# Third buffer of split weights, shared solve tiles, merge evictions after the weights, solved blocks copied on VectorE

## The chip, the cores and the metric

The kernel runs on one core of a Trainium2 chip. The metric is the device time of one execution in microseconds (us); three runs of the kernel before took 4509.4 to 4517.8 us, median 4514.72. Engines: PE is TensorE (PEld its weight loads), DVE VectorE, ACT ScalarE, POOL GpSimd, SP SyncE, which here issues most transfers.

## The reference, cut to what matters

Two layers over 256 context and 512 latent tokens of width 1024. Each layer has a mixer (one projection into three branches, a merge of the branches, an output projection) and an MLP. In the last layer only the latent tokens come out.

```
z = modulate(x) @ w_in                      # 10112 columns
A: r,k,v,decay,a = ...shifted, LoRA...      # RWKV-7, two directions, 16 heads of 64
   S = S*w_t - (S kk_t)(kk_t a_t)^T + v_t k_t^T;  y_t = S r_t
B: silu(layer_norm(depthwise_conv31(a * sigmoid(b))))
C: GQA, 8 query and 2 key heads of 128, softmax over context and latent keys
out = sum(sigmoid(z_gate) * (branch @ w_branch)) @ w_out
x = x + gate * rms_norm(out);  x = x + gate * rms_norm(relu(h @ w1)**2 @ w2)
```

## The kernel before

All matrices are float32. A product with a weight is made as three products of rounded parts. `weight_half` (L369) loads 512 rows by 128 columns of a weight into `raw`, ACT rounds it into a high part `wh` (L328), and the rest `raw - wh` becomes `wl`, on DVE (L332) or, in most of the mixer, on POOL (L330). Then `hh*wh + hl*wh + hh*wl` is summed in PSUM (`mm`). `raw` has two buffers (`nraw`), `wh` and `wl` have `nw` buffers.

In the mixer such products are jobs of eight steps in a queue; `fill` (L396, L412) takes out the next steps. The RWKV branch is written as generators, one yield per step, which `weave` runs in turn, letting `fill` put job steps between. Job steps thus fill PE while the branch waits for other engines. When `fill` starts a new half of a weight, it first issues halves until `ready` holds two. The tile framework then reorders the instructions of each engine, by their dependencies and the order in which they were issued; each engine runs its list in order.

The branch handles heads in pairs, eight per layer. For one pair: `rw_keys` writes the keys `BK`; `rw_front` the decayed `KR` and the Gram blocks `GL`, `GB`; `rw_rest` the solve's right hand sides `KM`; `rw_solve` (L855 to L864) inverts the triangular 32 x 32 blocks of all chunks on DVE and writes them to `Z` with two transposes (L863, L864). `rw_merge` joins blocks of 32 to blocks of 64, for each direction: PE multiplies (L892), ACT evicts with a minus sign (L896), ACT copies the solved blocks masked into `TT`, a view of `GL` (L900), PE multiplies again (L904), ACT evicts into `TT` (L906). `rw_batch` applies `TT` (L920, L931), `rw_chain` runs over the twelve chunks, `rw_readout` writes the output. The next pair's preparation, `prep`, runs beside it; `rw_bonus` has a key product (L877), whose operand DVE makes (L871).

`stage` (`f0`, one buffer) holds a finished job's copy: for the token shift (L654, L658) or on its way to DRAM (L1073 to L1076). `att_stats` loads ten stored tiles into `BK`, `KM` and `GL` in the layer's last pair and squares them (L544).

Of the kernel before, what the change touches and what calls it, by code (L numbers as in the profile page):

```python
# [8 lines left out]
F32 = mybir.dt.float32  # L9
# [3 lines left out]
AF = mybir.ActivationFunctionType  # L13
ALU = mybir.AluOpType
# [4 lines left out]
D = 1024  # L19
KT = 8  # L20
SEQ = 512
CTX = 256
TOK = CTX + SEQ
# [13 lines left out]
ROWS = (slice(0, 64), slice(64, 128))  # L37
# [39 lines left out]
class Kern:  # L77
# [247 lines left out]

    def split(s, hi, lo, src, pool=False):
        nc = s.nc
        nc.scalar.activation(out=hi, in_=src, func=AF.Copy)  # L328
        if pool:
            nc.gpsimd.tensor_tensor(out=lo, in0=src, in1=hi.bitcast(F32), op=ALU.subtract)  # L330
        else:
            nc.vector.tensor_tensor(out=lo, in0=src, in1=hi.bitcast(F32), op=ALU.subtract)  # L332
# [64 lines left out]
    def fill(s, n=1):  # L397
        nc = s.nc
        for _ in range(min(n, len(s.jobs))):
            k, mh, ml, T, done, pre = s.jobs.pop(0)  # L400
            if k % 4 == 0:
                while s.halves and len(s.ready) < 2:
                    s.ready.append(s.weight_half(*s.halves.pop(0)))
                s.cur = s.ready.pop(0)
            if k == 0:
                s.jps = s.mm()
                s.jctx = (pre(),) if pre else ()
            wh, wl = s.cur
            for w, m, f in ((wh, mh, 0), (wh, ml, 1), (wl, mh, 2)):
                a = m(k)  # L410
                for b, t0, t1 in s.pieces(T):
                    ins = nc.tensor.matmul(s.jps[:, b, :t1 - t0], lhsT=w[:, k % 4, :], rhs=a[:, t0:t1], start=k == 0 and f == 0, stop=k == KT - 1 and f == 2)  # L412
                    if s.pin and f == 0 and b == 0:
                        s.tc.keep_in_program_order(ins)
            if k == KT - 1:
                done(s.jps, *s.jctx)
# [112 lines left out]
    def att_stats(s, T, hold):  # L529

        nc = s.nc
        rs = s.ars = s.cp.tile([128, 2, 10, 6], F32, tag="ars", name="ars", bufs=1)
        slots = []
        for n in (('BK', 0), ('BK', 1), ('KM', 0), ('KM', 1), ('GL', 0)):
            t = s.big[n]
            t = t.rearrange({3: "p a b -> p (a b)", 4: "p a b c -> p (a b c)", 5: "p a b c d -> p (a b c d)"}[len(t.shape)])
            slots += [t[:, c:c + TOK] for c in range(0, t.shape[1], TOK)]
        heads = [8, 9] + list(range(8))
        for j, z in zip(heads, slots):
            s.zload(z, j, TOK if j > 7 else T)  # L540
        yield from hold
        for j, z in zip(heads, slots):
            o = 0 if j > 7 else TOK - T
            nc.scalar.activation(out=z[:, o:], in_=z[:, o:], func=AF.Square)  # L544
            cps = s.g([128, 6])
            for t in range(o // 128, 6):
                nc.tensor.matmul(cps[:, t:t + 1], lhsT=z[:, t * 128:t * 128 + 128], rhs=s.ones, start=True, stop=True)
            nc.vector.tensor_copy(rs[:, 0, j, o // 128:], cps[:, o // 128:])
            yield 1.4
        n0 = (TOK - T) // 128  # L550
        for h, t0 in ((slice(0, 8), n0), (slice(8, 10), 0)):
            nc.vector.tensor_scalar(out=rs[:, 0, h, t0:], in0=rs[:, 0, h, t0:], scalar1=1.0 / 128, scalar2=EPS, op0=ALU.mult, op1=ALU.add)
            u = slots[0][:, 0:60].rearrange("p (a b) -> p a b", b=6)
            s.rsqrt(rs[:, 0, h, t0:], rs[:, 1, h, t0:], u[:, h, t0:])
        q0, q1 = rs[:, 0, 0:8, n0:], rs[:, 1, 0:8, n0:]
        nc.vector.tensor_scalar(out=q0, in0=q0, scalar1=ATT_SCALE, scalar2=None, op0=ALU.mult)
        nc.vector.tensor_scalar(out=q1, in0=q0, scalar1=-1.0, scalar2=None, op0=ALU.mult)
# [87 lines left out]
        s.in_job(l, c0, T, lambda ps: s.shift_done(P, c0, T, dst(), ps))  # L645

    def stage(s):
        return s.wp.tile([128, TOK], F32, tag="f0", name="f0", bufs=1)

    def shift_done(s, P, c0, T, dst, ps):  # L650
        nc = s.nc
# [230 lines left out]

    def rw_merge(s, Q, d):

        nc = s.nc
        GL = s.big['GL', d]
        Dn, Dt = (s.Z[:, i:i + 384].rearrange("p (u t) -> p u t", t=32) for i in (1152 * d, 768 - 384 * d))
        one, two, c = (HI, LO, 0) if d else (LO, HI, 32)
        xp = s.g([128, 12, 32])
        for q in range(12):  # L890
            for h in range(2):
                nc.tensor.matmul(xp[two[h], q, :], lhsT=GL[one[h], h, q, c:c + 32], rhs=Dn[one[h], q, :], start=True, stop=True)  # L892
        TT = Q['TT', d] = GL.rearrange("p h c t -> p (h c t)")[:, 0:768].rearrange("p (c t) -> p c t", t=64)
        Xn = Dn
        for h in range(2):
            nc.scalar.activation(out=Xn[two[h]], in_=xp[two[h]], func=AF.Copy, scale=-1.0)  # L896
        yield 1.1 + s.sched['merge']
        for h in range(2):
            for o, m in ((0, s.tlo), (32, s.thi)):
                nc.scalar.activation(out=TT[ROWS[h], :, o:o + 32], in_=Dt[ROWS[h]], func=AF.Copy, scale=m[ROWS[h]])  # L900
        tr = s.g([128, 12, 32])
        for q in range(12):
            for h in range(2):
                nc.tensor.matmul(tr[one[h], q, :], lhsT=Xn[two[h], q, :], rhs=Dt[two[h], q, :], start=True, stop=True)  # L904
        for h in range(2):
            nc.scalar.activation(out=TT[one[h], :, c:c + 32], in_=tr[one[h]], func=AF.Copy, scale=-0.5)  # L906
        yield 1.1 + s.sched['merge']
# [170 lines left out]

    def run(s):
        nc, tc, i = s.nc, s.tc, s.i  # L1080
        s.nraw, s.nw, s.lo_pool, s.turn = 2, 2, False, 0
        s.halves, s.ready, s.jobs = [], [], []
        s.cops, s.pin = [], False
        s.psum('gen')
# [12 lines left out]
        with ExitStack() as xc:  # L1097
            X = xc.enter_context(tc.tile_pool(name="x0", bufs=1)).tile([128, KT, TOK], F32, name="X")
            sp = xc.enter_context(tc.tile_pool(name="n0", bufs=1))
            s.load_x(sp, X)  # L1100
            ss = s.ps2()
# [8 lines left out]
        for l in range(DEPTH):  # L1110
            T = TOK if l < DEPTH - 1 else SEQ
# [15 lines left out]
    def rwkv_phase(s, l, P, T):  # L1127
        nc, tc = s.nc, s.tc
        s.psum('rw')
        s.lo_pool = False  # L1130
        with ExitStack() as rc:
# [7 lines left out]
            for a, b in lay[3]:  # L1139
# [4 lines left out]
            s.X = s.A[:, 0:1024].rearrange("p (a b) -> p a b", b=32)  # L1144
            s.big = {(n, d): s.rp.tile(sh, F32, name=f"{n}{d}") for d in range(2) for n, sh in (
                ('BK', [128, 12, 2, 64]), ('KR', [128, 2, 12, 64]), ('GL', [128, 2, 12, 64]),
                ('GB', [128, 2, 12, 2, 64]), ('UV', [128, 24, 64]), ('KM', [128, 12, 2, 64]))}
            lat = T != TOK
            F = s.sched = SCHED[l]
            s.tdebt, s.tratio = 0.0, F['tap0']  # L1150
# [7 lines left out]
            def chain(*gs):  # L1158
                for g in gs:
                    yield from g  # L1160
            def prep(p, I, Q, *held):

                return chain(s.after(I, 'k', 0, s.rw_kk(P, p, I)), *held, s.rw_decay(P, p, Q), s.rw_keys(P, p, I, Q, 0), s.rw_keys(P, p, I, Q, 1),
                             s.after(I, 'r', 0, s.rw_bonus(P, p, I, Q, T)))

            def grams(I, Q, part):

                a, b = ((0, 0), (1, 2), (2, 1))[part]
                c = [slice(0, 8), slice(8, 12)] if part == 1 else [slice(0, 4), slice(8, 12)]
                gs = [s.rw_front(I, Q, 0, a, lat), s.rw_front(I, Q, 1, b, lat)]  # L1170
                if part == 1:
                    gs.append(s.rw_seed(0, slice(0, 8)))
                if part == 2:
                    gs += [s.rw_seed(1, slice(0, 12)), s.rw_seed(0, slice(8, 12))]
                return chain(*gs)
# [3 lines left out]
            I, In = {}, {}  # L1179
            s.rw_inputs(l, P, 0, T, I, 'krv')  # L1180
            s.fill(24)
            Q = s.rw_open(l, 0)
            s.pin = False
            spills(F['early'])
            s.weave(F['open'], prep(0, I, Q))
            s.conv_jobs(l, P, 0, T, s.ocv)
            s.weave(F['end'], chain(*(grams(I, Q, k) for k in range(3))))
            Qn = s.rw_open(l, 1)
# [6 lines left out]
            for p in range(8):  # L1195
                ev = set()

                def wait(*ns):
                    while not ev.issuperset(ns):
                        yield 0.0  # L1200
# [13 lines left out]
                held = [s.rw_readout(l, P, p - 1, old, T, s.orw), note('ro')] if old else [note('ro')]  # L1214
                gs = [chain(s.rw_merge(Q, 0), s.rw_batch(Q, 0, lat), note('b0'), wait('b1'), s.rw_chain(Q, lat, ev.add, wait('ro'))),
                      chain(s.rw_merge(Q, 1), s.rw_batch(Q, 1, lat), note('b1'))]
                if more:
                    gs.append(chain(prep(p + 1, In, Qn, *held), wait('s3'), grams(In, Qn, 0), wait('s7'), grams(In, Qn, 1), wait('s11'), grams(In, Qn, 2)))
                else:
                    gs.append(chain(*held, wait('s11'), s.rw_readout(l, P, p, Q, T, s.orw)))  # L1220
                    gs.append(chain(wait('b0', 'b1'), s.att_stats(T, wait())))
                s.weave(F['first'] if more else F['last'], *gs)
                s.taps(len(s.cops))
                if more:
                    s.conv_jobs(l, P, p + 1, T, s.ocv)
                    I, old, Q, In = In, Q, Qn, {}
                    if p < 6:
                        Qn = s.rw_open(l, p + 2)
# [106 lines left out]
    def mlp_phase(s, l, PP, T, acc, actx):  # L1335

        nc, tc, i, P = s.nc, s.tc, s.i, PP[l]
        o = TOK - T
# [12 lines left out]
        with tc.tile_pool(name="mlp", bufs=1) as sp:  # L1351
# [26 lines left out]
            if not last:  # L1378
                s.mod_pre(PP[l + 1])
                s.mod_post(PP[l + 1])  # L1380
            s.R = s.rstd(sp, ss, T, 1.0 / D, 0, CTX)
        with tc.tile_pool(name="n2", bufs=1) as sp:
            if last:
                s.post_norm(sp, acc, X, s.R, T, P['gm'][1], lambda k: None)
# [62 lines left out]
```

## Time and profile before

| | |
|---|---|
| profiled execution | 4503.07 us, span 4501.3 us |
| three runs | 4509.4, 4514.72, 4517.8 us |
| busy share of the span | PE 93%, PEld 76%, DVE 59%, ACT 42%, POOL 18% |
| granted PE clock, mean | 0.956 |
| mixer of layer 0, of layer 1 | about 130 to 1390 us, 2530 to 3710 us |

A row of waits says which engine sat idle before which line, and whose work ended the wait. In rows in order of time, the bracket is the idle time of the engine just before and who ended it. [...]

### The profile page before, as it was taken

The page shows a single profiled execution, that of the slowest core. Times are in us where ns is not written, and L with a number is a line of the kernel's source. Part 1 is how long each engine was busy: PE and PEld are TensorE (multiplying, and loading weights), DVE is VectorE, ACT ScalarE, POOL GpSimd, SP SyncE. Part 2 cuts the span into 40 slices and gives each one's busy share as a digit, 9 for nine tenths or more (in the row PEclk, how much of TensorE's full clock was granted, in tenths as well). Part 3 has the DMA queues.
Part 4 walks back from the last instruction along what each step waited for, and adds up shares of the span by engine and source line. Part 5 has one row for each costly group of instructions (what it writes and reads, how often), then busy time and mean ns, then how long its engine had stood idle before and what let it go on. Part 6 is the DMA issues. An engine that isn't in the chain of part 4 may idle for free. (4 is left out here: it accounts for less than half of the span.)

```text
span 4501.3 us, 76922 instructions
## 1 busy us (share of the span) xinstructions
PE 4197.0 (93%) x31232; PEld 3411.4 (76%) x31232; DVE 2642.9 (59%) x4762; ACT 1889.5 (42%) x3690; POOL 831.3 (18%) x737
## 2 busy tenths in 40 slices
PE   6999999999998989899999899999999988898998
PEld 4888888888786668689999667877777775475886
DVE  3788788887855443132233568778787845443344
ACT  3455445444534442232223354555555534434333
POOL 0011221212112144300000102122122212262001
PEclk8999999999999999999999889999999979998998
DMA  4211111111224234343322221111111223142332
GB/s 161 62 47 53 57 58 57 51 52 58 73 84 157 71 110 142 126 141 117 107 87 63 69 61 52 50 60 47 56 54 57 75 71 121 57 133 64 96 96 82
DMA packets 438346, 364.05 MB, mean 81 GB/s; under 512 B 19022, under 2 KB 386792, under 8 KB 431848
## 3 DMA queue, kind: packets, MB, share of 16 engines
q1 hardware_dynamic: 417256, 279.43, 20.5%
q10 hardware_dynamic: 20736, 79.70, 4.9%
q8 instruction: 247, 4.05, 0.4%
q14 instruction: 107, 0.88, 0.1%
HBM read 299.29 MB, written 53.48 MB: 78 GB/s over the span
## 5 line engine op out<-in xcount | busy, mean ns | idle before, releaser
L328 ACT ACTIVATE wh<-raw 128x512 fp32r<-128x512 f32 x700 | 441.4, 631 | 1261.5 <-PE mm L389 558.3
L330 POOL TENSOR_TENSOR wl<-raw,wh 128x512 fp32r<-128x512 f32 x388 | 535.5, 1381 | 2062.3 <-ACT wh L328 1699.1
L412 PE MATMUL mm<-hh,wh 128*128 128x384 f32 (+1 forms) x2072 | 668.6, 381 | 49.4 <-ACT wh L328 40.7
L412 PE MATMUL mm<-hl,wh 128*128 128x384 f32 (+1 forms) x2072 | 644.5, 370 | 7.0 <-POOL hl L330 7.0
L412 PE MATMUL mm<-hh,wl 128*128 128x384 f32 (+1 forms) x2072 | 641.4, 369 | 4.9 <-POOL wl L330 4.6
L332 DVE TENSOR_TENSOR wl<-raw,wh 128x512 fp32r<-128x512 f32 x312 | 215.5, 691 | 589.7 <-ACT wh L328 586.4
L412 PEld LDWEIGHTS mm<-hh,wh 128*128 128x128 f32 x2072 | 379.2, 195 | 112.7 <-ACT wh L328 45.6
L473 DVE SCALAR_TENSOR_TENSOR cv<-u,dw,cv 128x783 f32<-128x783 f32 (+1 forms) x480 | 458.3, 955 | 3.1
L412 PEld LDWEIGHTS mm<-hl,wh 128*128 128x128 f32 x2072 | 389.6, 195 | 47.7 <-issue 12.1
L412 PEld LDWEIGHTS mm<-hh,wl 128*128 128x128 f32 x2072 | 388.0, 194 | 47.1 <-POOL wl L330 10.8
L412 PE MATMUL mm<-oh,wh 128*128 128x384 f32 (+1 forms) x768 | 256.7, 389 | 12.1 <-DVE acc L1273 4.1
L412 PE MATMUL mm<-oh,wl 128*128 128x384 f32 (+1 forms) x768 | 245.9, 374 | 22.0 <-POOL wl L330 22.0
L412 PE MATMUL mm<-ol,wh 128*128 128x384 f32 (+1 forms) x768 | 243.5, 370 | 6.6 <-POOL ol L330 5.6
L389 PE MATMUL mm<-hh,wh 128*128 128x384 f32 (+1 forms) x768 | 239.3, 367 | 6.3 <-ACT hh L347 3.6
L389 PE MATMUL mm<-hl,wh 128*128 128x384 f32 (+1 forms) x768 | 238.3, 365 | 5.5 <-POOL hl L330 5.0
L389 PE MATMUL mm<-hh,wl 128*128 128x384 f32 (+1 forms) x768 | 236.0, 362 | 0.0
L389 PE MATMUL mm<-fh,wh 128*128 128x384 f32 (+1 forms) x768 | 230.2, 353 | 0.0
L389 PE MATMUL mm<-fh,wl 128*128 128x384 f32 (+1 forms) x768 | 230.0, 353 | 0.0
L389 PE MATMUL mm<-fl,wh 128*128 128x384 f32 (+1 forms) x768 | 229.8, 353 | 0.0
L862 DVE TENSOR_TENSOR A<-A,Z 128x30 f32<-128x30 f32 (+14 forms) x480 | 198.2, 413 | 15.8
L861 DVE TENSOR_TENSOR Z<-A 128x30 f32<-128x30 f32 (+14 forms) x480 | 190.7, 397 | 16.5
L412 PEld LDWEIGHTS mm<-oh,wh 128*128 128x128 f32 x768 | 143.9, 195 | 55.2 <-ACT wh L328 15.8
(294 smaller groups left out, 7425.6 us busy)
## 6 DMA issues: line engine op xcount, KB each, us to landing
raw<-in_w_in_dram SPq DMA_DIRECT2D x316, 256.0 KB
raw<-in_w_ff_dram SPq DMA_DIRECT2D x256, 256.0 KB
wmod<-in_w_mod_dram ACTq DMA_DIRECT2D x48, 1024.0 KB
raw<-in_w_branch_dram SPq DMA_DIRECT2D x96, 256.0 KB
z<-f ACTq DMA_DIRECT2D x40, 384.0 KB
gt<-z SPq DMA_DIRECT2D x24, 384.0 KB
raw<-in_w_out_dram SPq DMA_DIRECT2D x32, 256.0 KB
z<-f ACTq DMA_DIRECT2D x32, 256.0 KB
```

What stands on the lines that cost most here:

```text
L328: nc.scalar.activation(out=hi, in_=src, func=AF.Copy)
L330: nc.gpsimd.tensor_tensor(out=lo, in0=src, in1=hi.bitcast(F32), op=ALU.subtract)
L332: nc.vector.tensor_tensor(out=lo, in0=src, in1=hi.bitcast(F32), op=ALU.subtract)
L389: nc.tensor.matmul(ps[:, b, :t1 - t0], lhsT=w[:, k % 4, :], rhs=a[:, t0:t1], start=k == 0 and f == 0, stop=k == KT - 1 and f == 2)
L412: ins = nc.tensor.matmul(s.jps[:, b, :t1 - t0], lhsT=w[:, k % 4, :], rhs=a[:, t0:t1], start=k == 0 and f == 0, stop=k == KT - 1 and f == 2)
L473: s.tap_pin(nc.vector.scalar_tensor_tensor(out=hold['c'], in0=u[:, k:k + L], scalar=w(k), in1=hold['c'], op0=ALU.mult, op1=ALU.add))
L861: nc.vector.tensor_tensor(out=tm, in0=X[:, k + 1:, k:k + 1].to_broadcast([128, n, k]), in1=X[:, k:k + 1, 0:k].to_broadcast([128, n, k]), o ...
L862: nc.vector.tensor_tensor(out=X[:, k + 1:, 0:k], in0=X[:, k + 1:, 0:k], in1=tm, op=ALU.add)
```

## The change

`nw` is 3, and `fill` issues halves until `ready` holds `nw`. `split` keeps its last ACT instruction in `last_hi`; the evictions of a merge (now L895) get a dependency on it, which puts them behind it in ACT's order, without a semaphore. The masked copies into `TT` go from eight instructions of 64 partitions on ACT per pair to four of 128 partitions on DVE (L900 still). `KM` becomes the same tile as `BK`, and `prep` waits for each direction's batch (`b0`, `b1`) before it writes its keys; in a layer's first preparation that wait is empty. `stage` has two buffers. `att_stats` uses `BK`, `GL` and `A`. At the MLP's end the row of the norm uses the tag `sq`. Between `att_stats` and these copies, lines stand one lower than before: L891 is L892 of before, L895 is L896, L653 is L654, L862 and L863 are the transposes; the other lines named here keep their numbers.

```diff
     def split(s, hi, lo, src, pool=False):
         nc = s.nc
-        nc.scalar.activation(out=hi, in_=src, func=AF.Copy)
+        s.last_hi = nc.scalar.activation(out=hi, in_=src, func=AF.Copy)
...
             if k % 4 == 0:
-                while s.halves and len(s.ready) < 2:
+                while s.halves and len(s.ready) < s.nw:
...
-        for n in (('BK', 0), ('BK', 1), ('KM', 0), ('KM', 1), ('GL', 0)):
-            t = s.big[n]
...
+        for t in [s.big[n, d] for n in ('BK', 'GL') for d in range(2)] + [s.A]:
...
     def stage(s):
-        return s.wp.tile([128, TOK], F32, tag="f0", name="f0", bufs=1)
+        return s.wp.tile([128, TOK], F32, tag="f0", name="f0", bufs=2)
...
     def rw_merge(s, Q, d):
 
-        nc = s.nc
+        nc, hi = s.nc, s.last_hi
...
         for h in range(2):
-            nc.scalar.activation(out=Xn[two[h]], in_=xp[two[h]], func=AF.Copy, scale=-1.0)
+            ins = nc.scalar.activation(out=Xn[two[h]], in_=xp[two[h]], func=AF.Copy, scale=-1.0)
+
+            s.tc.add_manual_dep(ins.ins, hi.ins.name, mybir.DependencyInfo(mybir.DependencyClass.NoSync, mybir.DependencyReason.DATA), reason="weights first")
         yield 1.1 + s.sched['merge']
-        for h in range(2):
-            for o, m in ((0, s.tlo), (32, s.thi)):
-                nc.scalar.activation(out=TT[ROWS[h], :, o:o + 32], in_=Dt[ROWS[h]], func=AF.Copy, scale=m[ROWS[h]])
+        for o, m in ((0, s.tlo), (32, s.thi)):
+            nc.vector.tensor_scalar(out=TT[:, :, o:o + 32], in0=Dt, scalar1=m, scalar2=None, op0=ALU.mult)
...
-        s.nraw, s.nw, s.lo_pool, s.turn = 2, 2, False, 0
+        s.nraw, s.nw, s.lo_pool, s.turn = 2, 3, False, 0
...
-                ('GB', [128, 2, 12, 2, 64]), ('UV', [128, 24, 64]), ('KM', [128, 12, 2, 64]))}
+                ('GB', [128, 2, 12, 2, 64]), ('UV', [128, 24, 64]))}
+
+            s.big.update({('KM', d): s.big['BK', d] for d in range(2)})
...
-                return chain(s.after(I, 'k', 0, s.rw_kk(P, p, I)), *held, s.rw_decay(P, p, Q), s.rw_keys(P, p, I, Q, 0), s.rw_keys(P, p, I, Q, 1),
+                return chain(s.after(I, 'k', 0, s.rw_kk(P, p, I)), *held, s.rw_decay(P, p, Q), wait('b0'), s.rw_keys(P, p, I, Q, 0), wait('b1'), s.rw_keys(P, p, I, Q, 1),
```

How the order of instructions moves is seen at the merge of layer 1's second pair, first on ACT. `wh` are the weights' high parts, `f` and `in_k` the eviction of a finished job, `GL` the copies and second evictions of the merge, `Z` its first evictions. Before:

```order
L328 ACTIVATE wh<-raw 128x512 x3
L900 ACTIVATE GL_22444<-Z,cst 64x12x32 x3
L900 ACTIVATE GL_22438<-Z,cst 64x12x32 x3
L654 ACTIVATE f_24698<-mm 128x768
L655 ACTIVATE in_k<-mm,H 128x768
L328 ACTIVATE wh<-raw 128x512 x2
L900 ACTIVATE GL_22438<-Z,cst 64x12x32
L896 ACTIVATE Z<-g 32x384 x4
```

and now:

```order
L328 ACTIVATE wh<-raw 128x512 x4
L653 ACTIVATE f_24664<-mm 128x768
L654 ACTIVATE in_k<-mm,H 128x768
L328 ACTIVATE wh<-raw 128x512
L895 ACTIVATE Z<-g 32x384 x2
L713 ACTIVATE ksq<-in_k,V 128x768
L895 ACTIVATE Z<-g 32x384 x2
```

The copies are gone from ACT, and five high parts instead of three stand ahead of the first instruction that needs the solve's result.

On DVE at the same place, after the solve's last transposes (`Z`), now:

```order
L862 STREAM_TRANSPOSE Z<-A 128x32x32
L863 STREAM_TRANSPOSE Z<-A 128x32x32
L900 TENSOR_SCALAR GL_22409<-Z,cst 128x12x32
L900 TENSOR_SCALAR GL_22404<-Z,cst 128x12x32
L657 SCALAR_TENSOR_TENSOR in_k<-f_24664,H,in_k 128x255
L657 SCALAR_TENSOR_TENSOR in_k<-f_24664,H,in_k 128x511
L657 SCALAR_TENSOR_TENSOR in_k<-f_24664,H,in_k 128x255
L657 SCALAR_TENSOR_TENSOR in_k<-f_24664,H,in_k 128x511
L470 TENSOR_SCALAR cv<-u,dw,V 128x512
L900 TENSOR_SCALAR GL_22404<-Z,cst 128x12x32
L473 SCALAR_TENSOR_TENSOR cv<-u,dw,cv 128x512
L900 TENSOR_SCALAR GL_22409<-Z,cst 128x12x32
```

Two copies stand right behind the transposes, the other two behind the token shift of `in_k` and the first convolution tap; before, these rows stood without the L900.

On SP in layer 0's last pair, where `z` is what `att_stats` loads, now:

```order
L372 DMA raw<-in_w_in_dram 128x4x128 x5
L483 DMA GL_657<-z 128x768
L483 DMA A<-z 128x768 x2
L483 DMA GL_662<-z 128x768
L372 DMA raw<-in_w_in_dram 128x4x128 x2
L483 DMA GL_657<-z 128x768
L483 DMA GL_662<-z 128x768
```

Before, one load of `GL` stood between four and three loads of `raw`. The counts of big matmuls (`mm`) ahead of a place in PE's order move too: ahead of layer 0's first L877 26 more, of layer 1's first 14 more, of layer 0's last merge 12 more, of layer 1's last merge 20 fewer, and 3 + 3 between the halves of layer 1's first merge become 0 + 6.

## Rows read from the trace of the kernel before

**Rows 1.** Stretches, both mixer stages: length, busy us and count by engine, PEclk, DMA share, GB/s
```profile
130.00:1390.00 1260.00, 1213.37 (x11946) 1031.90 (x11945) 966.04 (x1764) 593.63 (x1252) 227.50 (x222) 0.98 0.20 62
...
2530.00:3710.00 1180.00, 1108.12 (x10289) 868.62 (x10289) 877.73 (x1692) 589.65 (x1249) 220.11 (x232) 0.92 0.19 58
```
**Rows 2.** Stretches, within layer 0's MLP
```profile
1990.00:2400.00 410.00, 410.00 (x2383) 390.00 (x2382) 121.64 (x161) 100.87 (x149) 1.70 (x4) 1.00 0.32 101
```
**Rows 3.** Waits of PE in layer 0's mixer: total us, times, longest
```profile
PE mm L412 <- ACT wh L328: 13.2, 7, 2.9
PE g L877 <- DVE key L871: 8.4, 5, 4.9
PE g L892 <- DVE Z L863: 4.8, 1, 4.8
```
**Rows 4.** Waits of PE in layer 1's mixer
```profile
PE mm L412 <- ACT wh L328: 27.5, 6, 7.9
PE g L892 <- DVE Z L863: 16.7, 3, 9.0
PE g L877 <- DVE key L871: 7.2, 2, 6.4
```
**Rows 5.** Waits of all engines, whole span
```profile
ACT GL L900 <- DVE Z L863: 102.7, 16, 9.0
```
**Rows 6.** Order of time, ACT, a merge of layer 1: start us, us, what [idle before]
```profile
2794.23 0.63 ACT L328 ACTIVATE wh<-raw 128x512 fp32r<-128x512 f32 x1 [3.42 <-PE mm L412]
2803.33 1.74 ACT L900 ACTIVATE GL<-Z,cst 64x384 f32<-64x384 f32 x3 [8.47 <-DVE Z L863]
...
2808.66 1.14 ACT L328 ACTIVATE wh<-raw 128x512 fp32r<-128x512 f32 x2
```
**Rows 7.** Order of time, PE, the same merge
```profile
2800.82 0.40 PE L412 MATMUL mm<-hl,wh 128*128 128x512 f32 x1
2801.05 0.40 PE L412 MATMUL mm<-hh,wl 128*128 128x512 f32 x1
2809.33 0.80 PE L412 MATMUL mm<-hh,wh 128*128 128x512 f32 x1 [7.88 <-ACT wh L328]
```
**Rows 8.** Order of time, DVE, the same merge
```profile
2801.39 1.91 DVE L863 STREAM_TRANSPOSE Z<-A 128x1024 f32<-128x1024 f32 x1
2803.33 1.92 DVE L864 STREAM_TRANSPOSE Z<-A 128x1024 f32<-128x1024 f32 x1
2808.80 4.23 DVE L658 SCALAR_TENSOR_TENSOR in_k<-f,H,in_k 128x255 f32<-128x255 f32 x4 [3.54 <-ACT in_k L655]
```
**Rows 9.** Stretches, right after that merge's gap
```profile
2809.30:2819.00 9.70, 9.10 (x112) 7.01 (x113) 6.44 (x7) 4.86 (x9) 3.12 (x2) 0.50 0.20 57
```
**Rows 10.** Order of time, PE, other waits of layer 1's mixer
```profile
2607.64 0.80 PE L412 MATMUL mm<-hh,wh 128*128 128x512 f32 x1 [3.68 <-ACT wh L328]
...
3210.41 0.79 PE L412 MATMUL mm<-hh,wh 128*128 128x512 f32 x1 [4.65 <-ACT wh L328]
...
3472.31 0.79 PE L412 MATMUL mm<-hh,wh 128*128 128x512 f32 x1 [7.08 <-ACT wh L328]
...
3614.09 1.49 PE L892 MATMUL g<-Z,GL 32*32 32x32 f32 x48 [9.03 <-DVE Z L863]
```
**Rows 11.** Order of time, PE, the first key product of each layer
```profile
164.47 2.29 PE L877 MATMUL g<-key,cst 128*128 128x384 f32 x3 [4.95 <-DVE key L871]
...
2615.25 2.07 PE L877 MATMUL g<-key,cst 128*128 128x512 f32 x2 [6.38 <-DVE key L871]
```
**Rows 12.** Groups by form, DVE: count | busy us, mean ns of one | idle before
```profile
L831 DVE TENSOR_SCALAR Z<-GL 32x384 f32<-32x384 f32 x64 | 28.6, 446 | 0.7
```
**Rows 13.** Order of time, POOL and DVE, a solve in layer 0
```profile
639.94 1.49 POOL L330 TENSOR_TENSOR wl<-raw,wh 128x512 fp32r<-128x512 f32 x1 [12.31 <-ACT wh L328]
...
640.32 1.36 DVE L861 TENSOR_TENSOR Z<-A 128x220 f32<-128x220 f32 x1
...
641.71 0.39 DVE L862 TENSOR_TENSOR A<-A,Z 128x220 f32<-128x220 f32 x1
```

More of the change, by code (lines that the diff above doesn't have):

```diff
@@ L533, in att_stats @@
         slots = []
-        for n in (('BK', 0), ('BK', 1), ('KM', 0), ('KM', 1), ('GL', 0)):
-            t = s.big[n]
-            t = t.rearrange({3: "p a b -> p (a b)", 4: "p a b c -> p (a b c)", 5: "p a b c d -> p (a b c d)"}[len(t.shape)])
+        for t in [s.big[n, d] for n in ('BK', 'GL') for d in range(2)] + [s.A]:
+            t = t.rearrange({2: "p a -> p a", 4: "p a b c -> p (a b c)"}[len(t.shape)])
             slots += [t[:, c:c + TOK] for c in range(0, t.shape[1], TOK)]
@@ L1160, in chain, with prep @@
                     yield from g
-            def prep(p, I, Q, *held):
-                return chain(s.after(I, 'k', 0, s.rw_kk(P, p, I)), *held, s.rw_decay(P, p, Q), s.rw_keys(P, p, I, Q, 0), s.rw_keys(P, p, I, Q, 1),
+            def prep(p, I, Q, wait, *held):
+                return chain(s.after(I, 'k', 0, s.rw_kk(P, p, I)), *held, s.rw_decay(P, p, Q), wait('b0'), s.rw_keys(P, p, I, Q, 0), wait('b1'), s.rw_keys(P, p, I, Q, 1),
                              s.after(I, 'r', 0, s.rw_bonus(P, p, I, Q, T)))
@@ L1184, in rwkv_phase @@
             spills(F['early'])
-            s.weave(F['open'], prep(0, I, Q))
+            s.weave(F['open'], prep(0, I, Q, lambda n: ()))
             s.conv_jobs(l, P, 0, T, s.ocv)
@@ L1217, in rwkv_phase @@
                 if more:
-                    gs.append(chain(prep(p + 1, In, Qn, *held), wait('s3'), grams(In, Qn, 0), wait('s7'), grams(In, Qn, 1), wait('s11'), grams(In, Qn, 2)))
+                    gs.append(chain(prep(p + 1, In, Qn, wait, *held), wait('s3'), grams(In, Qn, 0), wait('s7'), grams(In, Qn, 1), wait('s11'), grams(In, Qn, 2)))
                 else:
@@ L1380, in mlp_phase @@
                 s.mod_post(PP[l + 1])
-            s.R = s.rstd(sp, ss, T, 1.0 / D, 0, CTX)
+            s.R = s.rstd(sp, ss, T, 1.0 / D, 0, CTX, tag="sq")
         with tc.tile_pool(name="n2", bufs=1) as sp:
```

## The prediction

> **What bounds the kernel now.** I read the busy time by stage first, then who TensorE (PE) waits for, then the order of time at one place. In both mixer stages PE is busy nearly throughout: 1213.37 of 1260 us in layer 0 and 1108.12 of 1180 us in layer 1, at a granted clock of 0.98 and 0.92 [rows 1]. So 47 and 72 us are idle, and the lowered clock costs up to (1-0.98) x 1260 = 25 and (1-0.92) x 1180 = 94 us of full-speed time. In the MLP nothing is to be had: 410.00 of 410 us at 1.00 [rows 2]. That stretch also gives the price of a 384-column matmul, 410/2383 = 0.172 us; a 512-column one of layer 1 starts 0.23 us after the last [rows 7].
>
> Whom PE waits for: in layer 0 13.2 us for a weight's high part `wh` (7 waits), 8.4 us for the key product (one of 4.95), 4.8 us once for the solved blocks `Z` [rows 3]; in layer 1 27.5 us for `wh` (6 waits), 16.7 us for `Z`, 7.2 us for the key product [rows 4]. What lies behind the `wh` waits is seen on ScalarE (ACT): 16 times, once per merge, it is parked on L900 until VectorE (DVE) ends the solve, 102.7 us in all [rows 5].
>
> One merge of layer 1 shows the mechanism. ACT finishes a `wh` at 2794.9, then idles 8.47 us before its first L900; three copies and more work follow, and the next `wh` starts at 2808.66 [rows 6]. PE uses up what it has, stops at 2801.45, and resumes at 2809.33 after 7.88 us <-ACT wh [rows 7]. ACT is an in-order queue here: the `wh` that PE wants stands behind copies that wait for another engine. [...]
>
> **The change part by part.** Times are summed against the profiled execution, 4503.07 us (span 4501.3, 1.8 around it); the median of the three runs is 4514.72, 11.65 more, which I add at the end.
>
> *Copies to DVE, evictions behind `wh`.* ACT loses 128 L900 (one is 1.74/3 = 0.58 us [rows 6], some 74 us in all), and the order on ACT now has all `wh` of the lookahead ahead of the evictions. In layer 0 the 13.2 us of `wh` waits go: 13.2. PE does not meet the solve instead: of the eight merges there only one waits for `Z` [rows 3], and it is none of these seven.
>
> In layer 1 the six waits are priced one by one. Of 27.5 us, 3.68 lies ahead of the first key product (below), and 7.88, 4.65 and 7.08 are at merges [rows 7, 10]; the other two make 4.2. At the 7.88 one PE would go on from 2801.45 with three matmuls (0.7 us) and reach L892 at 2802.2. `Z` comes with L863 at 2803.30 and the second half with L864 at 2805.25 [rows 8]. So PE waits 1.1 us, and some 1.2 us more between the two halves of L892: 7.88 - 2.3 = 5.6 saved. The 7.08 one I take alike: 4.8. The 4.65 and the remaining 4.2 go whole, 8.9: layer 1's waits for `Z` are three [rows 4], at merges without a `wh` wait of several us, so I have no sign that PE meets the solve at these. Together 19.3.
>
> *Third buffer.* It lets the program hold three halves of weights ready, so more big matmuls stand ahead of waits. By the order, 26 more stand ahead of layer 0's first key product: 26 x 0.172 = 4.5 of the 4.95 us wait [rows 11]. In layer 1 it is 14 more: 14 x 0.23 = 3.2 of the 3.68 + 6.38 us there [rows 10, 11]. Ahead of layer 0's last merge stand 12 more (2.1 of the 4.8 us [rows 3]); ahead of layer 1's last merge 20 fewer, which lengthens its 9.03 us wait for `Z` [rows 10] by 20 x 0.23 = 4.6. The first merge of layer 1 loses the matmuls that filled its step from L892 to L904: 1 us. Net 4.5 + 3.2 + 2.1 - 4.6 - 1 = 4.2.
>
> Idle time saved: 13.2 + 19.3 + 4.2 = 36.7 us. In shares that is (13.2 + 4.5 + 2.1)/47 = 42% of layer 0's idle time and (19.3 + 3.2 - 4.6 - 1)/72 = 23% of layer 1's.
>
> *Clock.* If the low clock falls with the gaps, 42% of 25 and 23% of 94 us come back, 10.5 + 21.6 = 32. Some of it lies on idle time and would be counted twice, and not every low stretch need follow a gap. Bounds 0 and 32; I take two thirds, 21.
>
> *New costs.* 64 copies on DVE of 384 elements each. The nearest row is L831, 32 x 384, 446 ns [rows 12], so 64 x 0.45 = 29 us on DVE. It hides: after the solve DVE sits idle 3.54 us for `in_k` at that merge [rows 8], and two of the four copies of a merge stand in that hole. The later two wait for L891 to stop reading `GL`; behind them stand a convolution tap and the key norm, needed only after the merge. Bounds 0 and 29; I take 0. If the cover is gone, the 29 us stand on the path to the next pair's keys. An eviction that stands right behind a `wh` can lose one `wh`, 1.14/2 = 0.57 us [rows 6], at 16 merges: 0 to 9 us, I take 3. In each layer's last pair a load of `GL` now stands ahead of the copies of L906 on ACT: 0 to 4 us for both, I take 1.
>
> *Edits at nothing.* Keys in the solve operands' tile: in the order the key writes of the next pair already stood behind the batch that reads it; uncovered, it would be the wait for that batch. A second staging tile takes away waits of ACT for a transfer, not of PE: 0, at best a microsecond or two. The row tile's new tag: 0.
>
> Sum: 36.7 + 21 - 4 = 54 us; 4503.07 - 54 = 4449, and with 11.65 some 4461 us for the median. From the bounds (idle 25 to 42, clock 0 to 32, costs 0 to 13, and 29 at worst) its own range is a gain of 25 to 75, 4440 to 4490 us.
>
> **The rivals.** *The solve takes over.* The three long `wh` waits of layer 1 sit within some 2 us of the solve's end; if the rest do too, freed time turns into waits of L891 for `Z`. For it: 16.7 us of such waits already [rows 4]. Against it: layer 0. Left are 13.2 + 4.5 + 3.2 of idle, 8 of clock, less 4: gain 25, 4490 us.
>
> *It doesn't do what it says.* `raw` keeps two buffers, and if PE's `wh` waits are really for the load behind, ACT's freedom buys nothing. Against it: ahead of the copies ACT waits 3.42 us <-PE mm, for a `wh` buffer that PE has to free [rows 6], not for a load. Then 4515, within 9 us.
>
> *Slower: evictions held.* L895 must now follow the last `wh` issued. If that `wh`'s buffer is freed only by matmuls that stand at or behind L891, then L904 waits for one more half of weights: 24 x 0.172 = 4.1 us at 8 merges, 12 x 0.23 = 2.8 at 8, 55 us, and a dip of the clock after each. The 9.7 us at half speed [rows 9] cost 4.85; a third of that, 1.6, at 16 merges is 26. With the gains kept this gives 4461 + 81 = 4542 us; it decides from the point where that half stands behind L891. In the order it is complete ahead of L891 at all 16.
>
> *Slower or same: DVE and GpSimd (POOL) collide.* A DVE operation of 220 elements took 1.36 us while POOL ran a `wl` beside it, and its neighbour without one 0.39 [rows 13]. If each of the 64 copies meets a `wl` and pays 0.97 us, on the path, that is 62 us: 4523. The copies stand where PE eats its lookahead and `wl` runs, but DVE has idle time there, which speaks against the path. [...]
>
> **How the numbers follow.** Forecast 0.62; solve takes over 0.15; more than the forecast's range 0.05; does nothing 0.08; evictions held 0.06; collision 0.04. A measurement of this kernel tells 0.2%, 9 us, from no change. Faster: 0.62 + 0.15 + 0.05 = 0.82; same: 0.08 + 0.02 of the collision = 0.10; slower: 0.06 + 0.02 = 0.08. The range goes from the larger gain to the edge of no change: 4425 to 4508.
>
> **What would show it.** ACT should have no wait of several us at the merges for Z; PE's waits for `wh` should fall from 13.2 and 27.5 us to a few; waits of L891 for `Z` should rise by some 5 to 10 us in layer 1; the granted clock should rise to 0.99 and about 0.94; layer 0's first key product should wait under 1 us, the last merge of layer 1 some 13 us. I am wrong if `wh` waits stay, or if L904 waits for L895 by more than 2 us, or if DVE's wait for L891 delays the next keys.

## The result and the profile after

The changed kernel takes 4455.83 us (median of four runs, 4442.7 to 4456.46), the kernel before beside it 4515.36 (4509.4 to 4517.8): a ratio of 0.9863, 95% interval 0.9843 to 0.9884. The profiled execution took 4455.6 us, 47.5 less than the one before; both have a mean granted clock of 0.956 (the share of full speed that PE got; at any time of the two traces it is 1.00 or 0.50). I cut both spans at the first L523 (the attention's first product) and the first L389 (the MLP's first product) after each mixer, and at the MLP's last L389; layer 0's mixer is counted from 130.0 and 128.5 us. Stage lengths in us:

| | before | after | gain |
|---|---|---|---|
| layer 0: mixer | 1256.5 | 1239.1 | 17.4 |
| layer 0: merge of the branches (first L523 to first L389) | 526.2 | 512.7 | 13.5 |
| layer 1: mixer | 1221.5 | 1210.1 | 11.4 |
| all the rest | | | 5.2 |

The mixers first, the stretches that answer to [rows 1], then layer 0's merge phase:

```profile
128.50:1371.00 1242.50, 1215.11 (x11943) 1037.03 (x11943) 981.50 (x1796) 558.23 (x1188) 233.91 (x222) 0.98 0.20 63
2498.00:3665.00 1167.00, 1108.61 (x10290) 875.51 (x10290) 892.55 (x1724) 553.46 (x1185) 221.92 (x232) 0.92 0.20 58
1367.60:1880.20 512.60, 470.55 (x2332) 361.74 (x2332) 214.55 (x379) 201.57 (x360) 175.28 (x115) 0.97 0.38 124
```

PE's idle time falls from 46.6 to 27.4 us in layer 0 and from 71.9 to 58.4 in layer 1; its busy time does not fall at all, and the clock stays at 0.98 and 0.92. So the gain in the mixers is idle time alone. Whom PE waits for in layer 0 now, against [rows 3]:

```profile
PE g L891 <- DVE Z L862: 5.9, 1, 5.9
PE g L876 <- DVE key L870: 4.0, 4, 2.2
PE g L716 <- ACT Z L895: 2.3, 1, 2.3
```

and in layer 1, against [rows 4] (total us, times, longest):

```profile
PE g L891 <- DVE Z L862: 29.3, 7, 7.6
PE g L716 <- ACT Z L895: 4.5, 2, 2.8
PE g L876 <- DVE key L870: 4.4, 2, 3.7
PE g L891 <- DVE Z L863: 4.0, 6, 1.4
...
PE mm L412 <- ACT wh L328: 2.8, 2, 1.9
```

The `wh` waits are gone in layer 0 and down from 27.5 to 2.8 us in layer 1. There the waits for `Z` have nearly doubled, to 29.3 + 4.0 = 33.3 us. Before they were 16.7 for the first transpose [rows 4] and 1.2 for the second, 17.9 in all:

```profile
PE g L892 <- DVE Z L864: 1.2, 2, 0.7
```

PE is no longer stopped ahead of the solve's end by ACT, so it arrives earlier at the solve's end and waits there. The second pair's merge, whose rows of before are [rows 6 to 8], shows it. ACT, in order of time:

```profile
2773.76 0.63 ACT L328 ACTIVATE wh<-raw 128x512 fp32r<-128x512 f32 x1 [0.79 <-issue]
2779.40 0.97 ACT L895 ACTIVATE Z<-g 32x384 f32<-32x384 f32 x2 [5.00 <-PE g L891]
2782.41 0.94 ACT L713 ACTIVATE ksq<-in_k,V 128x768 f32<-128x768 f32 x1 [2.04 <-DVE in_k L657]
2783.37 0.97 ACT L895 ACTIVATE Z<-g 32x384 f32<-32x384 f32 x2
```

PE:

```profile
2774.22 0.39 PE L412 MATMUL mm<-hh,wl 128*128 128x512 f32 x1
2777.87 1.49 PE L891 MATMUL g<-Z,GL 32*32 32x32 f32 x48 [3.26 <-DVE Z L862]
2779.82 1.49 PE L891 MATMUL g<-Z,GL 32*32 32x32 f32 x48 [0.46 <-DVE Z L863]
```

Before, PE stopped for 7.88 us for `wh`. Now it is not short of weights: a `wh` was ready at 2774.39, and the L412 behind the merge runs without a wait. But L891 stands next in PE's order, and it waits 3.72 us for the two transposes. ACT is not free of parking either: in layer 1 L713 waits 24.0 us for DVE's L657 (4.6 us before the change). The clock after the shorter wait, and at the third pair's merge, where PE waits for nothing:

```profile
2908.00:2928.00 20.00, 20.00 (x282) 17.95 (x281) 9.23 (x25) 9.26 (x16) 5.67 (x4) 1.00 0.24 69
2779.80:2790.00 10.20, 10.10 (x163) 8.39 (x163) 7.58 (x24) 3.37 (x7) 0.00 (x0) 0.50 0.01 2
```

A granted 0.50 comes with the 3.72 us as it came with the 7.88 us [rows 9]: it lasts from 2777.2 to 2794.3 us now, from 2805.3 to 2819.0 before. The third pair's merge proves no gain: its longest wait before was 0.63 us, and no half speed followed it then either (1.00 from 2825.8 to 3078.4 us). A wait that is gone whole is seen in layer 0. Ahead of the seventh pair's merge PE waited 2.64 us for `wh`, until 1104.91; now it does not wait there. The stretch before (granted 0.83), then the one ahead of that merge now (1.00):

```profile
1103.00:1113.00 10.00, 7.97 (x36) 7.47 (x37) 1.60 (x4) 5.45 (x9) 3.85 (x3) 0.83 0.19 54
```
```profile
1085.00:1103.00 18.00, 17.88 (x237) 17.24 (x236) 13.56 (x24) 6.66 (x12) 4.52 (x3) 1.00 0.21 60
```

There the low clock went with the wait; over the whole mixers no such gain shows, 0.98 and 0.92 as before.

### The profile page after: what moved, and what is told of

Read it like the earlier page. It is cut to its first block, busy times and chain, and to the rows that moved or that the text cites. A ratio compares the mean times of both kernels' runs of the same rounds, so it can differ in the third digit from the quotient of the medians.

```text
span 4453.8 us, 76934 instructions
## 1 busy us (share of the span) xinstructions
PE 4190.7 (94%) x31232; PEld 3412.5 (77%) x31232; DVE 2674.6 (60%) x4828; ACT 1817.7 (41%) x3562; POOL 837.4 (19%) x735
## 5 line engine op out<-in xcount | busy, mean ns | idle before, releaser
L330 POOL TENSOR_TENSOR wl<-raw,wh 128x512 fp32r<-128x512 f32 x386 | 534.2, 1384 | 2008.5 <-ACT wh L328 1697.7
L412 PE MATMUL mm<-hh,wh 128*128 128x384 f32 (+1 forms) x2072 | 668.1, 381 | 11.6 <-ACT hh L347 4.0
L412 PE MATMUL mm<-hl,wh 128*128 128x384 f32 (+1 forms) x2072 | 647.9, 371 | 7.0 <-POOL hl L330 7.0
L412 PE MATMUL mm<-hh,wl 128*128 128x384 f32 (+1 forms) x2072 | 641.9, 369 | 0.0
L412 PEld LDWEIGHTS mm<-hh,wh 128*128 128x128 f32 x2072 | 381.1, 195 | 70.5 <-issue 19.0
L412 PEld LDWEIGHTS mm<-hl,wh 128*128 128x128 f32 x2072 | 390.2, 195 | 46.2 <-issue 10.5
L412 PEld LDWEIGHTS mm<-hh,wl 128*128 128x128 f32 x2072 | 391.1, 195 | 38.5 <-issue 12.1
L412 PE MATMUL mm<-oh,wh 128*128 128x384 f32 (+1 forms) x768 | 252.4, 383 | 11.2 <-DVE acc L1275 5.8
L412 PE MATMUL mm<-ol,wh 128*128 128x384 f32 (+1 forms) x768 | 240.0, 365 | 11.6 <-POOL ol L330 11.6
L389 PE MATMUL mm<-hh,wh 128*128 128x384 f32 (+1 forms) x768 | 238.5, 365 | 6.3 <-ACT hh L347 3.6
L412 PE MATMUL mm<-oh,wl 128*128 128x384 f32 (+1 forms) x768 | 240.0, 365 | 2.3 <-POOL wl L330 2.2
L389 PE MATMUL mm<-hl,wh 128*128 128x384 f32 (+1 forms) x768 | 236.7, 362 | 5.8 <-POOL hl L330 5.3
L389 PE MATMUL mm<-hh,wl 128*128 128x384 f32 (+1 forms) x768 | 234.8, 361 | 0.0
L389 PE MATMUL mm<-fh,wh 128*128 128x384 f32 (+1 forms) x768 | 230.2, 353 | 0.0
L389 PE MATMUL mm<-fh,wl 128*128 128x384 f32 (+1 forms) x768 | 230.0, 353 | 0.0
L389 PE MATMUL mm<-fl,wh 128*128 128x384 f32 (+1 forms) x768 | 229.8, 353 | 0.0
L860 DVE TENSOR_TENSOR Z<-A 128x30 f32<-128x30 f32 (+14 forms) x480 | 202.5, 422 | 16.6
L412 PEld LDWEIGHTS mm<-oh,wh 128*128 128x128 f32 x768 | 140.1, 190 | 56.0 <-ACT wh L328 12.8
```

The source lines that it names most:

```text
L389: nc.tensor.matmul(ps[:, b, :t1 - t0], lhsT=w[:, k % 4, :], rhs=a[:, t0:t1], start=k == 0 and f == 0, stop=k == KT - 1 and f == 2)
L860: nc.vector.tensor_tensor(out=tm, in0=X[:, k + 1:, k:k + 1].to_broadcast([128, n, k]), in1=X[:, k:k + 1, 0:k].to_broadcast([128, n, k]), o ...
```

## The experiments

Theory A: ACT parked on the copies is what cost. Theory B: the third buffer carries nearly all. Each result has its ratio to the kernel before on the same chip.

**Two buffers.**

```diff
-        s.nraw, s.nw, s.lo_pool, s.turn = 2, 3, False, 0
+        s.nraw, s.nw, s.lo_pool, s.turn = 2, 2, False, 0
```

> The changed kernel with nw = 2 again; the copies on VectorE and the evictions behind the high parts stay. Theory A (the third buffer gives only the first key products and, in layer 0's merge phase, the waits of POOL's low parts; ScalarE's freedom gives the mixers' gain): about 4485 to 4490 us, against 4456 of the changed kernel and 4515 of the one before; waits of PE for wh in the mixers a few us more than now, the wait for wl in layer 0's merge phase back at about 10 us. Theory B (the third buffer alone carries nearly all; the copies matter little): 4505 to 4515 us, with 13 and 27 us of wh waits back.

4469.88 us, 0.9899 (0.9881 to 0.9917). The time lies below both ranges, nearer to A: the third buffer is worth only 14 us. Layer 0's mixer takes 1237.5 us, layer 1's mixer and merge phase together 1601.4 (changed kernel 1239.1 and 1601.5): their length shows nothing, though the first key products wait up to 4.9 and 6.4 us again (1.0 and 3.7 in the changed kernel). Of the 19.8 us between the two profiled executions 18.6 lie in layer 0's merge phase. The stretch of the kernel before, of this run and of the later one with a lookahead of two:

```profile
1386.50:1912.70 526.20, 478.09 (x2333) 371.57 (x2333) 213.00 (x379) 201.72 (x361) 175.25 (x116) 0.96 0.37 121
```
```profile
1366.00:1897.30 531.30, 480.82 (x2333) 371.23 (x2333) 212.70 (x379) 201.88 (x361) 174.98 (x116) 0.95 0.37 120
```
```profile
1372.50:1884.70 512.20, 472.97 (x2333) 364.60 (x2333) 213.30 (x380) 201.32 (x360) 176.47 (x115) 0.97 0.39 124
```

and the wait that goes, in the kernel before:

```profile
PE mm L412 <- POOL wl L330: 10.1, 4, 4.6
```

With two buffers it is 12.3 us, with three 1.0. The intervals of this run and of the changed kernel just touch; the phase tells them apart. With the low parts on POOL it takes 526 to 532 us in the four traces with two buffers and 511 to 516 in the seven with three. In layer 1's merge phase such waits fall too (12.0 to 1.2 us), but it takes 391.8 us before and 391.4 after.

**Copies on ACT again.**

```diff
-        for o, m in ((0, s.tlo), (32, s.thi)):
-            nc.vector.tensor_scalar(out=TT[:, :, o:o + 32], in0=Dt, scalar1=m, scalar2=None, op0=ALU.mult)
+        for h in range(2):
+            for o, m in ((0, s.tlo), (32, s.thi)):
+                nc.scalar.activation(out=TT[ROWS[h], :, o:o + 32], in_=Dt[ROWS[h]], func=AF.Copy, scale=m[ROWS[h]])
```

> The changed kernel with the copies into TT on ScalarE again (eight instructions of 64 partitions per pair); third buffer and the order of the evictions stay. Theory A: ScalarE is parked on L900 again and the wh waits return in part: 4475 to 4485 us, PE's wh waits above 15 us in layer 1. Theory B: with three buffers PE rides over the parking: 4453 to 4460 us, wh waits of a few us.

4476.66 us, 0.9918 (0.9899 to 0.9937): A by the time, neither by the mechanism. With three buffers no `wh` wait returns (2.8 us in layer 1, as in the changed kernel); ACT is parked as before (53.1 us in layer 1), and PE now waits for the key norm that stands behind the copies, for which the changed kernel has no wait in layer 1. In layer 0 L716 waits 13.0 us for ACT, against 4.6. In layer 1:

```profile
ACT GL L901 <- DVE Z L862: 53.1, 8, 9.1
...
PE g L716 <- ACT ksq L713: 9.4, 3, 4.4
```

**No order for the evictions** (the line with `add_manual_dep` is taken out).

> The changed kernel without the dependency that puts the merge's evictions behind the last high part issued. Theory A: evictions that wait for PE's merge product stand ahead of one or two high parts, PE waits for wh by some 5 to 10 us in layer 1, 4460 to 4468 us. Theory B: the third buffer covers that, and without the dependency L895 no longer waits behind L713 and the high parts, so that the 2 to 3 us waits of L716 for L895 go: 4450 to 4456 us.

4456.02 us, 0.9871 (0.9855 to 0.9886): B. The dependency is worth nothing here, and it is not what delays L895 either: L716 still waits 6.8 us for it, three times. ACT stands at L713, which waits for DVE's L657.

**Third buffer and shared tiles alone** (the two edits above together).

> The changed kernel with the copies on ScalarE and without the dependency: the third buffer and the shared tiles by themselves. Theory A: 4480 to 4495 us (layer 0's merge phase and the first key products keep their gain, some 20 us; the wh waits at the merges of layer 1 return). Theory B: 4455 to 4465 us.

4486.26 us, 0.9939 (0.9921 to 0.9958): A by the time, not by its mechanism. Layer 0's mixer is back at 1254.5 us, its merge phase stays at 512.0. But the `wh` waits of layer 1 do not return (2.8 us); PE waits there 10.9 us for the key norm behind the copies, as in the run with the copies on ACT.

**Copies alone**, in the kernel before (the second diff's first two lines in place of its last three).

> The kernel before with one edit: the copies into TT go to VectorE (four of 128 partitions per pair). Theory A (ScalarE parked on the copies is what cost, the order of the evictions, the shared tiles and the second staging tile are nothing): the time of the run with two buffers, 4466 to 4474 us, wh waits of PE in the mixers some 8 us in all. Rival (the evictions have to stand behind the high parts for that gain, since with two buffers an L896 that waits for PE stands ahead of a high part): 4485 to 4500 us, wh waits above 20 us.

4462.38 us, 0.9886 (0.9859 to 0.9912): A, a little below its range. With this edit alone only 3.7 us of `wh` waits are left in layer 1. Its interval overlaps those of the changed kernel and of the one with two buffers: order, shared tiles and second staging tile can't be told from nothing. By the time alone nor can the third buffer; it shows in layer 0's merge phase, which takes 531.6 us here.

**More job steps in the solve** (`solve=48` for `solve=40` in layer 1's row of the schedule).

> The changed kernel with 48 instead of 40 job steps put between layer 1's solves and what follows (the total of steps is the same). Theory C (in layer 1 the end of the solve is now the limit, and each merge that waits for it also pays about 8.5 us of lowered clock): the 33 us of waits of L891 for Z fall under 10, and the clock's loss in that mixer falls from about 100 to 60 us or less where the waits vanish wholly: 4400 to 4440 us. Rival D (the steps are missing elsewhere: what is moved to the solve is taken from the chain of the pair, where PE then waits for VectorE and ScalarE): 4450 to 4480 us, L891's waits gone and other waits of the same size in their place.

4452.62 us, 0.9868 (0.9843 to 0.9893). It doesn't decide: counted in the traces, between a solve's start and its merge stand 122 big matmuls on average in the changed kernel and 124 in this one; the reordering leaves them where they were, and the waits for `Z` stay (38.2 us in layer 1, against 33.3). But it shows something else. Up to layer 1 the instruction lists of all engines are those of the changed kernel, and PE's waits in layer 0's mixer agree to a few tenths; yet that mixer ends 10 us earlier. The first L523 of the changed kernel and of this one:

```profile
1367.58 1.96 PE L523 MATMUL g<-kraw,rope 128*128 128x512 f32 x4 [1.60 <-DVE kT L583]
```
```profile
1357.48 1.96 PE L523 MATMUL g<-kraw,rope 128*128 128x512 f32 x4 [1.82 <-DVE kT L583]
```

The next run, with the same lists in layer 0, has it at 1358.58. These 10 us are the granted clock's (0.98 against 0.99 in that stretch): its share differs from run to run of the same instructions. The changed kernel's own four runs had 0.956 three times, and 0.961 in the one of 4442.7 us.

**Low parts on DVE in layer 1.**

```diff
-            s.lo_pool = True
+            s.lo_pool = l == 0
```

> The changed kernel with layer 1's low parts wl of the mixer on VectorE instead of GpSimd. It asks whether the solves of layer 1, which take 2 us longer than before the change (some 37 instead of 35 us), are slowed by GpSimd's low parts beside them. If so, the solve's own instructions take their time of before again or less (the 128x220 operations 0.4 us, none above 1 us). If not, they stay as they are. The time itself: VectorE gets some 150 operations of 0.69 us in layer 1, a part of them ahead of the solve's end, 4460 to 4520 us.

4408.39 us, 0.9761 (0.9742 to 0.9781), 47 us less than the changed kernel, outside what I expected of the time. The question is answered with yes: the longest of the solves' operations in layer 1 takes 0.41 us. POOL and then DVE of the changed kernel, in one solve of layer 1:

```profile
2754.91 1.29 POOL L330 TENSOR_TENSOR wl<-raw,wh 128x512 fp32r<-128x512 f32 x1 [1.87 <-ACT wh L328]
2757.72 1.29 POOL L330 TENSOR_TENSOR wl<-raw,wh 128x512 fp32r<-128x512 f32 x1 [1.53 <-ACT wh L328]
```
```profile
2755.04 1.42 DVE L861 TENSOR_TENSOR A<-A,Z 128x234 f32<-128x234 f32 x1
2756.50 0.41 DVE L860 TENSOR_TENSOR Z<-A 128x238 f32<-128x238 f32 x1
2756.94 0.41 DVE L861 TENSOR_TENSOR A<-A,Z 128x238 f32<-128x238 f32 x1
2757.38 0.41 DVE L860 TENSOR_TENSOR Z<-A 128x240 f32<-128x240 f32 x1
2757.83 1.46 DVE L861 TENSOR_TENSOR A<-A,Z 128x240 f32<-128x240 f32 x1
```

The operation that starts while a `wl` runs ends just after it (2756.46 against 2756.20) and takes 1 us more. Over the whole trace 88 of the 960 operations of the solves start so; they take 1.33 us on average, the others 0.33, and 86 of them end behind the `wl`, in the median 0.24 us. The solve's two lines in layer 1, grouped (count | busy us, mean ns | idle before), first the kernel before, then the changed one, then this run:

```profile
L862 DVE TENSOR_TENSOR A<-A,Z 128x30 f32<-128x30 f32 (+14 forms) x240 | 102.5, 427 | 7.8
L861 DVE TENSOR_TENSOR Z<-A 128x30 f32<-128x30 f32 (+14 forms) x240 | 96.3, 401 | 8.1
```
```profile
L861 DVE TENSOR_TENSOR A<-A,Z 128x30 f32<-128x30 f32 (+14 forms) x240 | 104.9, 437 | 7.9
L860 DVE TENSOR_TENSOR Z<-A 128x30 f32<-128x30 f32 (+14 forms) x240 | 104.7, 436 | 8.2
```
```profile
L861 DVE TENSOR_TENSOR A<-A,Z 128x30 f32<-128x30 f32 (+14 forms) x240 | 79.4, 331 | 6.9
L860 DVE TENSOR_TENSOR Z<-A 128x30 f32<-128x30 f32 (+14 forms) x240 | 79.1, 329 | 7.3
```

198.8, 209.6 and 158.5 us: the collisions cost 40 us in layer 1 before the change and 51 after it, 6.4 us a solve. In this run PE waits for `Z` 6.2 us in layer 1 instead of 33.3, and that mixer takes 1178.5 us. That DVE makes a `wl` in half the time (0.69 against 1.38 us) is no rival there: in layer 1's mixer of the changed kernel PE waits for no `wl`. Of the 52 us between the two profiled executions 32 lie in that mixer and 12 in layer 1's merge phase, whose `wl` are on DVE too and where collisions and the faster `wl` are not told apart; 9 lie in layer 0's mixer and are the clock's, as in the run before.

**Lookahead of two, three buffers** (`fill` issues halves until two are ready).

> The changed kernel with three buffers of wh and wl, but halves issued only until two are ready, as before. It asks what of the third buffer does the work in layer 0's merge phase. If it is the lookahead in the order of issue: that phase takes 526 to 531 us as with two buffers, 4467 to 4472 us. If it is the buffer that PE need not free first: 513 us and 4453 to 4460 us.

4444.56 us, 0.9845 (0.9823 to 0.9866). It is the buffer: 512.2 us in the merge phase, shown above. The time lies below both ranges. Whether it beats the changed kernel is not settled, the intervals overlap.

**Low parts on DVE in both layers** (`s.lo_pool = False`).

> The changed kernel with the mixer's low parts wl on VectorE in both layers. Theory E (the solve's end matters only where PE waits for it): layer 0's solves get some 5 us shorter too, but only its last merge waits for one (5.9 us), so its mixer gains at most 6 us (1224 to 1240 us against 1229 to 1239); its merge phase, where PE waits for POOL's low parts ol, gains 5 to 12 us; in all 4395 to 4406 us. Rival (VectorE, with 0.69 us more for each of some 160 halves, is late with the keys in layer 0, whose pairs hold more matmul work per pair): above 4412 us.

4375.72 us, 0.9693 (0.9673 to 0.9713): the best time but one, and below both ranges. Layer 0's merge phase gains 11.3 us (501.4), as Theory E had it; the mixer gains more than it allowed. Layer 0's mixer falls to 1209.7 us, 1213.1 in a stretch that answers to [rows 1]:

```profile
128.50:1341.60 1213.10, 1200.56 (x11949) 1024.73 (x11948) 970.52 (x1928) 558.33 (x1188) 46.17 (x90) 0.99 0.21 64
```

Idle time falls by 14.9 us, not by the one wait for `Z`: the first key product's waits (4.0 to 1.0 us) and others end earlier too, it seems because all that DVE does comes earlier. PE's busy time falls by 14.5 us, of which some 10 lie within the clock's scatter. DVE itself, with 132 more instructions in that stretch, is busy 11 us less there than in the changed kernel (981.50). Over the whole span it is busy 38 us more, 2712.8 against 2674.6.

**Low parts on DVE in layer 1, kernel before.**

> The kernel before with layer 1's low parts wl of the mixer on VectorE, nothing else. Theory F (GpSimd's low parts slowed the solve before the change as well, and a shorter solve shortens ScalarE's parking on L900): the solves of layer 1 fall from about 35 to 32 us or less, the 27.5 us of wh waits and 16.7 us of Z waits there shrink by half: 4470 to 4490 us. Rival (the collision only became a loss when ScalarE was freed and the low parts moved beside the solve): 4505 to 4520 us.

4488.32 us, 0.9938 (0.9913 to 0.9962): F by the time. The `wh` waits of layer 1 fall from 27.5 to 8.3 us and those for `Z` nearly go (0.6 us left); but PE now waits 9.9 us for DVE's `wl`. The mixer gains 3 us in its profile and the merge phase 10.5. The same edit is worth 29 us here (4517.45 to 4488.32 on the same chip) and 47 on the changed kernel.

**Both, and a lookahead of two.**

> The changed kernel with the mixer's low parts on VectorE in both layers and halves issued only until two are ready. If the gain of the lookahead of two (4444.6 against 4456) is one of the mechanism, it adds to that of the low parts: 4385 to 4396 us. If it was the scatter of the granted clock from run to run: the time of the run with low parts on VectorE in both layers, within 5 us.

4372.6 us, 0.9685 (0.966 to 0.9709): 3 us from the run before it, so the lookahead of two adds nothing that shows.

**Low parts on DVE, two buffers.**

> The changed kernel with the mixer's low parts on VectorE in both layers and two buffers of wh and wl again. Theory G (the third buffer was worth its 14 us because a low part takes GpSimd 1.38 us and PE waited for it; VectorE takes 0.69 us): layer 0's merge phase stays at 501 to 506 us, and the time at 4373 to 4382 us, against 4375.7 with three buffers. Rival (PE's hold on two buffers is what cost, whoever makes the low part): that phase takes 512 to 520 us, 4388 to 4400 us.

4412.62 us, 0.9775 (0.9755 to 0.9795). Theory G falls, and the rival by the place of the loss: the merge phase takes 509.3 us, and the time is 37 us worse than with three buffers, most of it in the mixers (1227.3 and 1190.0 us against 1209.7 and 1179.4). In layer 1:

```profile
PE g L876 <- DVE key L870: 10.7, 4, 6.4
PE mm L412 <- DVE wl L332: 7.0, 4, 5.9
PE mm L412 <- ACT wh L328: 6.3, 3, 3.7
```

DVE makes a `wl` between its other work (PE waits up to 5.9 us for one, which takes 0.69), and PE needs a half more in hand: with three buffers its waits for `wl` in layer 1's mixer are 0.2 us, with two 7.0.

## Why the prediction was right, and where it was not

The time was right, 4455.83 against 4461 in 4425 to 4508, but not by the sum that led to it. The mixers were to give all 54 us and gave 17.4 + 11.4 = 28.8; 13.5 came from a stage that the sum left out. The copies' term and the new costs held, the third buffer's held in part, the clock's failed.

*Copies and order.* Right on the copies: the `wh` waits went, and with the copies alone they go too. The idle time gained is 46.6 - 27.4 = 19.2 us in layer 0, where the terms made 19.8, and 13.5 in layer 1, where they made 16.9. The order half of the step is refuted: without the dependency the time is the same.

*"In layer 1 the six waits are priced one by one."* Half wrong. I took 4.65 and 4.2 us to go whole, having no sign that PE meets the solve there. It meets it at seven of eight merges; of the 24.7 us of `wh` waits that went, 15.4 came back as waits for `Z`, where I had said 5 to 10. I had called this the rival "the solve takes over"; in layer 1 it is what happened, and in layer 0 not.

*Third buffer, "net 4.2".* The first key products came as said: they wait 1.0 and 3.7 us instead of 4.95 and 6.38, and with two buffers 4.9 and 6.4 again. The last merges did not: layer 0's waits 5.9 us for `Z`, not 4.8 - 2.1, and layer 1's 7.6, not 9.0 + 4.6. In the length of the mixers the buffer shows nothing. Its 13.5 us are in layer 0's merge phase, whose 10.1 us of PE's waits for `wl` I did not look at, since I read the mixers and the MLP only.

*Clock, 21.* This step failed. PE's busy time is unchanged in both mixers. I let the clock's cost shrink with the length of the gaps. But in layer 1 the low stretch after 3.72 us is no shorter than the one after 7.88 us (17.1 against 13.7 us), and seven of eight merges there still wait. Where a wait went whole, in layer 0, half speed went with it, too little to show: 10 us of a mixer is what the clock differs by itself. The missing 21 and the unforeseen 13.5 are of opposite sign, and the 11.65 us added at the end did not come, as the changed kernel's profiled run stands at its median (4455.6 and 4455.83): the forecast was near partly by luck.

*New costs.* The copies are as cheap as said, 406 ns against 0.45 us, and hidden:

```profile
L900 DVE TENSOR_SCALAR GL<-Z,cst 128x384 f32<-128x384 f32 x64 | 24.3, 406 | 19.9 <-PE g L891 19.8
```

One by one, in ns (shortest, median, longest), they take:

```profile
L900 DVE TENSOR_SCALAR GL<-Z,cst x64: 330/405/1021, 220.1 to 3575.5; 128x384 f32<-128x384 f32 x64
```

DVE stands 19.8 us for L891 ahead of these copies, but the next keys are not late: the key products wait less than before (8.4 to 4.0 and 7.2 to 4.4 us). Only two of the 64 copies start while POOL runs an L330. One starts 0.46 us into it and takes 1.02 us; the other starts at its end and takes 0.37. The longest of the remaining 62 takes 0.42. So a copy collides too, as the prediction's rival had it, but hardly ever. That rival was right that an operation which starts beside a `wl` takes longer, and had the wrong victim: not the copies but the solve, slowed so before the change too (1.36 against 0.39 us [rows 13]). ACT, set free, lets `wl` run more beside the solve, 198.8 to 209.6 us (200.8 with the copies on ACT again), 1.4 us for each of eight solves, on the path in layer 1. The 4 us for late evictions and a late load show in no run by themselves; L716's waits for ACT's evictions rose from 2.3 to 6.8 us.

*What would show it.* ACT's waits for the solve at L900 are gone and `wh` fell, as said; the clock did not rise. Layer 0's first key product waited 1.0 us where I said less; layer 1's last merge 7.6 us, not 13. ACT still waits several us at merges, but at L713 for DVE's L657. L716, ahead of L904 in PE's order, did wait up to 2.8 us for L895, the sign I gave for held evictions, but the dependency is not its cause.

## What to carry to other kernels

When a wait of the busiest engine is removed, write down what ends next at that place, instance by instance, and do not count the low clock as gone because the wait is shorter (here 0.50 came after 3.72 us as after 7.88). Read every stage in which a resource that the change enlarges is used, not only those where the complaint was. PE, too, ran its list in order here: with weights at hand it stood 3.72 us at a product whose operand was late. Work put on GpSimd to relieve VectorE can cost VectorE more than it would take there (in layer 0's mixer DVE is busy 981.50 us with the low parts on POOL and 970.52 with them on itself): look for operations of one shape with two durations, and see what ran beside the long ones.

## What was not expected of the hardware

A 128x512 subtraction takes POOL 1.38 us and DVE 0.69, but each solve operation that starts beside it on POOL takes about 1.0 us more. With all of the mixer's and the merge phase's low parts on DVE, DVE is busy 11 us less in layer 0's mixer (38 us more over the whole span), and the kernel takes 80 us less (4455.83 to 4375.72); the collisions are a part of these 80 us, not all of them. The same instruction lists in layer 0's mixer took 1239.1, 1229.0 and 1230.1 us in three executions, with PE's waits equal to a few tenths: the granted clock made 10 us of difference.
